# Down projection in stages of 4 plain tiles and 16 tiles by Strassen pairs, a last stage by token halves, and a final scaling by four tiles at a time

## The chip, the cores and the metric

The kernel runs on one core of one Trainium2 chip. The metric is the device time in microseconds (us) of one execution. A core has five engines that run their own instruction queues: TensorE (PE; its weight loads are listed as PEld), VectorE (DVE), ScalarE (ACT), GpSimd (POOL) and SyncE (SP, which here only issues transfers). All transfers run on 16 shared DMA engines.

## The reference

One layer of an encoder over 512 tokens of width 2048 in float32. The change touches only its last step, the SwiGLU feed-forward part with 5632 hidden features and the normalization behind it:

```python
u = rms_norm(h, ffn_pre_g[l])
gate, up = jnp.split(u @ w_gate_up[l], 2, axis=-1)
f = (jax.nn.silu(gate) * up) @ w_down[l]
h = h + rms_norm(f, ffn_post_g[l])
```

`rms_norm` divides each token by the root of its mean square and multiplies by a gain per feature. The output is float32, (1, 512, 2048).

## The kernel before

Activations are held transposed: a tile has 128 features on the partitions and 512 tokens along it. So the hidden activations are 44 tiles (`FT`), the output is 16 tiles (`KT`). `A` and `B` are the first and the last 256 tokens.

**Products of three terms.** Each float32 operand is split into a rounded part `hi` (a ScalarE cast) and the rest `lo` (a VectorE subtraction). A product of one weight tile and one activation tile is three matmuls: hi by lo, hi by hi, lo by hi (`gemm`, lines 179, 182 and 183, whose weights come through `wchunk`, lines 131 to 133). Activations are split by `split` (line 142).

**Pairs.** `strassen` makes two output tiles over 16 contraction tiles at once, by seven products of half size in place of eight (Strassen's scheme in Winograd's form). The operands on the activation side, `op`, are 56 tiles that `prepare` makes: `merged` puts the hi and lo parts of a half side by side (lines 155 and 156), so that the hi weights take one matmul of 512 columns (line 262) and the lo weights one of 256 (line 264). The weights come as four quarters on SP's queue, and one sum of quarters is built by an accumulating DMA on GpSimd's queue (`sums`, line 227). `behind_last` is a function that is called behind the last of the seven products, and the copy of the second result (`done`) then comes behind it.

**Storage.** Tiles named `slot` come from a pool of 66 buffers, weights from three small pools (`raw` 5 buffers, `whi` and `wlo` 3 each), and PSUM has 8 banks (`bank` and `abank`, 4 each). The program is written in order, and a planner orders each engine's instructions from that order and its own estimates; `tc.keep_in_program_order` holds an instruction to the written order on its engine. Waits are made by the framework.

**The work around the change.**
1. Lines 826 to 846 make the hidden tiles 5 to 43 by pairs of gate and up. `activated` stores each tile to `a_d`; for tiles 4 to 19 it also sums their squares (line 796, on GpSimd). At tile 21 the reciprocal root per token is made (`rstd`, then `by_column`, which spreads it over the partitions) as `arow`, its inverse as `irow`. `scaled` loads one of the tiles 4 to 19, multiplies it by `arow` on GpSimd and stores it to `as_d`, so that the pairs' differences work on numbers of one size; one call per tile, from 22 to 37.
2. Plain tiles 0 to 3, for all 16 outputs (`pd0`): a copy of each result (`yf`, line 877, three buffers) is stored to `y_d` from ScalarE's queue. `prepare` runs beside it and loads the scaled tiles (`load_rows`, line 856).
3. Eight pairs over tiles 4 to 19; `added` multiplies each result by `irow` on GpSimd (line 887) and adds it to `y_d` with an accumulating DMA (line 888).
4. Plain tiles 20 to 43, 14 outputs, two at a time (`pd1`): the sum so far is loaded from `y_d` and added on VectorE (line 934), and the squares of the result are summed.
5. The last two outputs in two token halves (`products`, tile names `pl` and `wl`). While the second half's products run, the first half is normalized and stored: `r4` is the reciprocal root, `normalized` (line 956) multiplies by it and by the gain, then h (`ha`, loaded in four-tile and two-tile pieces) is added on GpSimd or VectorE (line 985).
6. The second half: for each two outputs, two multiplications on VectorE from PSUM (line 956), one addition of `hb` (line 997) and one store on SP's queue (line 998).

Of the kernel before, what the change touches and what calls it, by code (L numbers as in the profile page):

```python
# [50 lines left out]
DN_F = 4  # L51
DN_S = DN_F + KT
DN_R = FT - DN_S
# [7 lines left out]
EARLY, EARLY_AT, MORE = 3, 2, 5  # L61
# [6 lines left out]
def hybrid_block(ctx: ExitStack, tc, xT, vecs, rpb, mask, w_c0, w_qk, w_v, w_gg, w_cg, w_ao, w_co, w_out, w_g0, w_gu, w_dn, outT):  # L68
# [717 lines left out]
    asum = const.tile([P, NT], F32, name="asum")  # L786
# [28 lines left out]
    as_d = dr.tile([KT, P, NT], F32, name="as_d")  # L815
    y_d = dr.tile([KT, P, NT], F32, name="y_d")
    arow, irow = asum, const.tile([P, NT], F32, name="irow")

    def scaled(k):

        t = slot(f"an{k}")
        nc.gpsimd.dma_start(t, a_d[DN_F + k])
        nc.gpsimd.tensor_tensor(out=t, in0=t, in1=arow, op=ALU.mult)  # L823
        nc.gpsimd.dma_start(as_d[k], t)

    for j in range(5, FT):
        if j == FT - EARLY_AT:
            acts = [load(k) for k in range(EARLY)]
        c11, c12, c21, c22 = strassen(w_gu[j], w_gu[FT + j], op, f"f{j}", j)
# [16 lines left out]
        activated(j, t)  # L846


    b11, b2, b_t12, b_t34 = [], [], [], []

    rows = []

    def load_rows(c):
        rows.append([slot(f"da{c}_{n}") for n in range(2)])
        for n, t in enumerate(rows[c]):
            nc.gpsimd.dma_start(t, as_d[c + n * HT])

    def prepare(c):

        if c + 2 < HT:  # L860
            load_rows(c + 2)
        u1, u2 = rows[c]
        b11.append(merged(u1[:, A], f"d11_{c}"))
        b2.append([merged(u2[:, cols], f"d2{c}_{n}") for n, cols in enumerate((A, B))])
        tt = stp.tile([P, 2, NT], F32, tag="S", name=f"dt{c}")
        winograd_t(u1, u2, tt[:, 0], tt[:, 1])
        b_t12.append([merged(tt[:, 0, cols], f"d12{c}_{n}") for n, cols in enumerate((A, B))])
        b_t34.append([merged(tt[:, 1, cols], f"d34{c}_{n}") for n, cols in enumerate((A, B))])

    acts += [load(k) for k in range(EARLY, DN_F)]  # L870
    for c in range(2):
        load_rows(c)
    for o in range(KT):
        ps = (bank, abank)[o % 2](f"pd0_{o}")
        gemm([(ps, w_dn[o])], acts, f"wd0_{o}", n=DN_F, pin=o < 2)
        t = stp.tile([P, NT], F32, tag="quad", name=f"yf{o}", bufs=3)
        nc.scalar.copy(t, ps)
        nc.scalar.dma_start(y_d[o], t)
        if o % 2 == 0:
            prepare(o // 2)  # L880


    op = operands(b11, b2, b_t12, b_t34)

    def added(ys):
        for o, t in ys:
# [3 lines left out]
    def split_first():  # L890
        acts.extend(split(t, f"fa{DN_S + k}", pin=True) for k, t in enumerate(first))

    acts = []
    for o in range(0, KT, 2):
# [11 lines left out]
        if o < KT - 2:  # L906
            added(ys)
# [176 lines left out]
```

## Time and profile before

| | |
|---|---|
| three runs, median (lowest to highest) | 2552.57 us (2551.17 to 2553.13) |
| the profiled execution | 2550.88 us |
| its span, first to last instruction | 2549.1 us |
| granted TensorE clock, mean | 0.994 of full |
| moved by DMA | 430.32 MB, 169 GB/s over the span |

The span is one execution as the hardware profiler recorded it. Busy times count instructions, so a busy TensorE can still be one whose matmuls run at a lower clock or wait inside. In the timeline a row is the start, the duration, the engine, the line, the operation with its output and inputs, and the count when several were merged; in brackets stand the idle time before it and what ended it. A matmul's duration is longer than the distance to the next matmul's start, because matmuls overlap; the distance is what one costs in a row of many.

### The profile page before, as it was taken

How to read it: one execution, taken by the hardware profiler on the slowest of the kernel's cores; microseconds unless marked ns; L12 is line 12 of the kernel's file. 1: busy time of each engine (PE TensorE's matmuls, PEld its weight loads, DVE VectorE, ACT ScalarE, POOL GpSimd, SP SyncE). 2: the span in 40 equal slices, each digit the busy share in tenths (PEclk: the TensorE clock that was granted, in tenths of full speed). 3: DMA queues.
4: the chain of work that ended last, by engine and by line, in shares of the span. 5: the costliest groups of instructions: out<-in, count | busy, mean ns of one | idle time of the engine just before them, and what ended most of it. 6: DMA issues, size and time to landing. Idle time of an engine off the chain costs nothing.

```text
span 2549.1 us, 34640 instructions
## 1 busy us (share of the span) xinstructions
PE 2513.1 (99%) x13207; PEld 2158.5 (85%) x13207; DVE 1867.8 (73%) x2412; ACT 1123.1 (44%) x1652; POOL 341.5 (13%) x383
## 2 busy tenths in 40 slices
PE   9999999999999999999999999999999999999997
PEld 7888888878888888889988888888888878878887
DVE  5999896577776655338798888788888888873326
ACT  5223333455554422225455555555555575452222
POOL 0110222220000011001101111112110012330002
PEclk9999999999999999999999999999999999999998
DMA  6246333476667445227356656676666577773335
GB/s 210 91 147 200 107 96 101 157 242 191 189 182 250 153 134 190 97 94 223 103 150 178 184 168 171 180 212 206 199 193 191 175 241 198 185 261 109 115 116 165
DMA packets 143910, 430.32 MB, mean 169 GB/s; under 512 B 16896, under 2 KB 24192, under 8 KB 143744
## 3 DMA queue, kind: packets, MB, share of 16 engines
q1 hardware_dynamic: 102144, 324.32, 38.5%
q0 software_dynamic: 22016, 69.22, 12.7%
q10 hardware_dynamic: 19584, 34.58, 3.7%
q8 instruction: 103, 1.69, 0.3%
q14 instruction: 63, 0.52, 0.1%
HBM read 371.95 MB, written 49.28 MB: 165 GB/s over the span
## 4 chain that ended last, share of the span: by engine, by line
PE 85%; DVE 8%; issue 3%; DMA 2%; ACT 1%; POOL 1%; ACTq 0%; SPq 0%; DVEq 0%; POOLq 0%
PE f L262 19%; PE f L264 10%; PE g L262 7%; PE d L262 4%; PE g L264 4%; PE pd L183 3%; PE pd L179 3%; PE pd L182 3%; PE qk L183 2%; PE qk L182 2%; PE qk L179 2%; PE po L183 2%; PE po L182 2%; PE po L179 2%; PE py L179 2%
## 5 line engine op out<-in xcount | busy, mean ns | idle before, releaser
L408 DVE SCALAR_TENSOR_TENSOR cv<-z,vec,cv 128x497 f32<-128x497 f32 (+14 forms) x240 | 190.7, 796 | 4.8
L133 DVE TENSOR_TENSOR wlo_wd<-raw_wd,whi_wd 128x1024 fp32r<-128x1024 f32 (+1 forms) x58 | 64.2, 1110 | 110.8 <-ACT whi_wd L132 109.4
L132 ACT CAST whi_wd<-raw_wd 128x1024 fp32r<-128x1024 f32 (+1 forms) x58 | 54.0, 934 | 166.5 <-PE pd L182 121.3
L133 DVE TENSOR_TENSOR wlo_wo<-raw_wo,whi_wo 128x1024 fp32r<-128x1024 f32 x36 | 47.4, 1318 | 106.6 <-ACT whi_wo L132 106.5
L132 ACT CAST whi_wo<-raw_wo 128x1024 fp32r<-128x1024 f32 x36 | 37.9, 1054 | 130.0 <-PE po L182 122.7
L320 POOL TENSOR_TENSOR r_r<-r_v,mhalf 128x2 f32<-128x2 f32 (+1 forms) x6 | 7.0, 1174 | 488.7 <-DVE r_v L318 438.2
L132 ACT CAST whi_y<-raw_y 128x1024 fp32r<-128x1024 f32 x32 | 33.5, 1051 | 79.4 <-PE py L182 76.2
L132 ACT CAST whi_qk<-raw_qk 128x1024 fp32r<-128x1024 f32 x32 | 33.7, 1052 | 77.1 <-PE qk L182 56.5
L133 DVE TENSOR_TENSOR wlo_qk<-raw_qk,whi_qk 128x1024 fp32r<-128x1024 f32 x32 | 40.3, 1260 | 32.3 <-ACT whi_qk L132 32.1
L133 DVE TENSOR_TENSOR wlo_y<-raw_y,whi_y 128x1024 fp32r<-128x1024 f32 x32 | 53.3, 1667 | 10.8 <-ACT whi_y L132 9.9
L665 DVE TENSOR_TENSOR gg<-py,gg 128x512 f32<-128x512 f32 x32 | 21.9, 690 | 52.7 <-PE py L183 52.7
L796 POOL TENSOR_TENSOR asum<-asum,asq 128x512 f32<-128x512 f32 x15 | 19.9, 1328 | 237.9 <-ACT asq L795 237.9
L183 PE MATMUL py<-ych,wlo_y 128*128 128x512 f32 x128 | 49.8, 389 | 0.0
L182 PE MATMUL py<-ych,whi_y 128*128 128x512 f32 x128 | 49.8, 389 | 0.0
L179 PE MATMUL py<-ycl,whi_y 128*128 128x512 f32 x128 | 49.8, 389 | 0.0
L842 ACT ACTIVATE sg<-sg 128x512 f32<-128x512 f32 x39 | 24.7, 634 | 50.9 <-DVE sg L300 50.9
L489 POOL TENSOR_TENSOR bm<-braw,msk 128x128 f32<-128x128 f32 x56 | 41.9, 781 | 15.4 <-DMA braw<-in_rpb 15.3
L934 DVE TENSOR_TENSOR y<-pd,y 128x512 f32<-128x512 f32 x14 | 9.7, 691 | 41.6 <-PE pd L183 38.8
L823 POOL TENSOR_TENSOR an<-an,asum 128x512 f32<-128x512 f32 x16 | 25.5, 1594 | 103.8 <-DMA an<-a_d 101.9
L887 POOL TENSOR_TENSOR ys<-ys,irow 128x512 f32<-128x512 f32 x16 | 27.1, 1692 | 76.6 <-PE d L262 41.6
L161 PE MATMUL f<-b,whi_f 128*128 128x256 f32 x128 | 36.4, 285 | 0.8 <-DVE b L156 0.8
L162 PE MATMUL f<-b,whi_f 128*128 128x256 f32 x128 | 36.2, 283 | 0.0
(3077 smaller groups left out, 8492.6 us busy)
## 6 DMA issues: line engine op xcount, KB each, us to landing
raw_wd<-in_w_dn SPq DMA_DIRECT2D x42, 512.0 KB, 3.7
raw_wo<-in_w_out SPq DMA_DIRECT2D x36, 512.0 KB, 3.9
raw_qk<-in_w_qk SPq DMA_DIRECT2D x32, 512.0 KB, 3.7
a_d<-sg ACTq DMA_DIRECT2D x44, 256.0 KB, 3.8
raw_v<-in_w_v SPq DMA_DIRECT2D x16, 512.0 KB, 4.3
raw_y<-in_w_ao SPq DMA_DIRECT2D x16, 512.0 KB, 3.8
gg<-g_d SPq DMA_DIRECT2D x32, 256.0 KB, 4.2
raw_y<-in_w_co SPq DMA_DIRECT2D x16, 512.0 KB, 3.5
```

The costliest lines, as they stand in the source:

```text
L132: cast(hi[:, s], raw[:, s])
L133: nc.vector.tensor_tensor(out=lo[:, s], in0=raw[:, s], in1=hi[:, s].bitcast(F32), op=ALU.subtract)
L161: nc.tensor.matmul(o, hi, t[:, B], start=first, stop=False, skip_group_check=True)
L162: nc.tensor.matmul(o, hi, t[:, A], start=False, stop=False, skip_group_check=True)
L179: mmul = nc.tensor.matmul(ps, hi[:, s], al, start=first, stop=False)
L182: nc.tensor.matmul(ps, hi[:, s], ah, start=False, stop=False)
L183: nc.tensor.matmul(ps, lo[:, s], ah, start=False, stop=last)
L262: nc.tensor.matmul(ps, hi[:, ws[k]], t, start=first and k == 0, stop=False, skip_group_check=True)
L264: nc.tensor.matmul(ps[:, A], lo[:, ws[k]], t[:, A], start=False, stop=last and k == HT - 1, skip_group_check=True)
L408: nc.vector.scalar_tensor_tensor(out=a[:, to], in0=z[:, fr], scalar=col(C_WDW, i * CW + w), in1=a[:, to], op0=ALU.mult, op1=ALU.add)
L489: nc.gpsimd.tensor_tensor(out=bm[:, o + i - i0], in0=raw[:, :, i * BC : (i + 1) * BC], in1=msk[:, o + i - i0, None, :].broadcast_to([P, RO ...
L887: tc.keep_in_program_order(nc.gpsimd.tensor_tensor(out=t, in0=t, in1=irow, op=ALU.mult))
```

## The change

- The hidden tiles go through the down projection in five stages: 0 to 3 plainly, 4 to 19 by pairs, 20 to 23 plainly, 24 to 39 by pairs, 40 to 43 by token halves for all 16 outputs.
- Both groups of 16 are scaled, each by its own rows: two sums of squares (`row[0]`, `row[1]`), two reciprocal roots, two inverses. Of the 32 `scaled` calls 22 stand beside the hidden tiles, 10 in the first pairs, two per pair.
- The plain stage and the making of the pairs' operands are one function, `products_and_operands`, called twice. In the second call a result is added to `y_d` by an accumulating DMA on GpSimd's queue; in the first it is stored as before.
- `added` runs at the head of the next pair or stage, and the first three activation tiles of each plain stage are loaded two pairs ahead and split behind the last product of the pair before.
- The last stage: for each two outputs the weights of tiles 40 to 43 are one DMA, split once into slots and used for both halves. Both outputs of a half share one PSUM bank. The squares of the sums are added up over the outputs in halves. In the second half ScalarE also multiplies each result by its gain (`yg`).
- The final scaling multiplies four tiles at a time by the row in PSUM, adds `hb` for two tiles at a time and stores on two queues.

```diff
+DN_P = 4
+DN_A = (DN_P, DN_P + KT)
+DN_2 = DN_P + 2 * KT
+DN_3 = DN_2 + DN_P
...
     def activated(j, t):
         nc.scalar.dma_start(a_d[j], t)
-        if j == DN_F:
-            nc.scalar.activation(asum, t, AF.Square)
-        elif DN_F < j < DN_S:
-            sq = slot(f"asq{j}")
-            nc.scalar.activation(sq, t, AF.Square)
-            nc.gpsimd.tensor_tensor(out=asum, in0=asum, in1=sq, op=ALU.add)
+        for n, k0 in enumerate(DN_A):
+            if j == k0:
+                nc.scalar.activation(row[n], t, AF.Square)
+            elif k0 < j < k0 + KT:
+                sq = slot(f"asq{j}")
+                nc.scalar.activation(sq, t, AF.Square)
+                nc.gpsimd.tensor_tensor(out=row[n], in0=row[n], in1=sq, op=ALU.add)
...
+    def early(k0):
+        raw = [load_raw(k0 + k) for k in range(EARLY)]
+        return lambda: acts.extend(split(t, f"fa{k0 + k}", pin=True) for k, t in enumerate(raw))
...
-        if j == DN_S + 1:
-            ra, va = rstd([asum], KT * P, "ra", eps=TINY)
-            nc.scalar.copy(arow, by_column(ra, "ra"))
-            ia = const.tile([P, NB], F32, name="ia")
-            nc.vector.tensor_tensor(out=ia, in0=va, in1=ra, op=ALU.mult)
-            nc.scalar.copy(irow, by_column(ia, "ia"))
-        if DN_S + 2 <= j < DN_S + 2 + KT:
-            scaled(j - DN_S - 2)
+        for n, k0 in enumerate(DN_A):
+            if j == k0 + KT + 1:
+                ra, va = rstd([row[n]], KT * P, f"ra{n}", eps=TINY)
+                ia = const.tile([P, NB], F32, name=f"ia{n}")
+                nc.vector.tensor_tensor(out=ia, in0=va, in1=ra, op=ALU.mult)
+                inverse.append(ia)
+            elif j == k0 + KT + 2:
+                nc.scalar.copy(row[n], by_column(ra, f"ra{n}"))
+        if DN_A[0] + KT + 2 <= j < DN_A[1] + KT + 2:
+            scaled(j - DN_A[0] - KT - 2)
+        elif j >= DN_A[1] + KT + 2:
+            if j == DN_A[1] + KT + 3:
+                nc.scalar.copy(row[0], by_column(inverse[0], "ia0"))
+            scaled(j - DN_A[0] - KT - 2)
...
+    def products_and_operands(n, k0, add):
...
+        acts.extend([load(k0 + k) for k in range(EARLY, DN_P)])
+        for c in range(2):
+            load_rows(c)
+        added()
+        for o in range(KT):
+            ps = (bank, abank)[o % 2](f"pd{n}_{o}")
+            gemm([(ps, w_dn[o, :, k0 * P : (k0 + DN_P) * P])], acts, f"wd{n}_{o}", n=DN_P, pin=o < 2)
+            t = stp.tile([P, NT], F32, tag="quad", name=f"yf{o}", bufs=3)
+            nc.scalar.copy(t, ps)
+            if add:
+                nc.gpsimd.dma_start(y_d[o], t, accum_op=ALU.add)
+            else:
+                nc.scalar.dma_start(y_d[o], t)
+            if o % 2 == 0:
+                prepare(o // 2)
...
+    def pairs(n, op, k0):
+        for o in range(0, KT, 2):
+            added()
+            if o == KT - 4:
+                behind = early(k0)
+            w0, w1 = (w_dn[o + i, :, DN_A[n] * P : (DN_A[n] + KT) * P] for i in range(2))
+            c11, c12, c21, c22 = strassen(w0, w1, op, f"d{n}_{o}", o // 2, behind_last=behind if o == KT - 2 else None)
+            for _ in range(2 if left else 0):
+                scaled(left.pop(0))
...
+    pairs(0, products_and_operands(0, 0, False), DN_2)
+    nc.scalar.copy(row[1], by_column(inverse[1], "ia1"))
+    pairs(1, products_and_operands(1, DN_2, True), DN_3)
...
+    def weights(o):
+        raw = wraw(f"wl{o}").rearrange("p (n k) -> p n k", n=2)
+        nc.sync.dma_start(raw, w_dn[o : o + 2, :, DN_3 * P :].rearrange("n p k -> p n k"))
+        for i in range(2):
+            w.append(split(raw[:, i], f"wl{o + i}"))
+            y.append(slot(f"y{o + i}"))
+            load_in_order(y[o + i], y_d[o + i])
+
+    def half(n, between={}):
+        cols, other = ((A, B), (B, A))[n]
+        acc = None
+        for o in range(0, KT, 2):
+            if n == 0:
+                weights(o)
+            ps = (bank, abank)[o // 2 % 2](f"pl{n}_{o}")
+            sq = slot(f"ysq{n}_{o}")
+            for i, part in enumerate((other, cols)):
+                hi, lo = w[o + i]
+                for k in range(DN_P):
+                    s = slice(k * P, (k + 1) * P)
+                    ah, al = (t[:, cols] for t in acts[k])
+                    for wt, t in ((hi, al), (hi, ah), (lo, ah)):
+                        nc.tensor.matmul(
+                            ps[:, part], wt[:, s], t, start=k == 0 and t is al, stop=k == DN_P - 1 and wt is lo,
+                            skip_group_check=True,
+                        )
+            between.get(o, lambda: None)()
+            for i, part in enumerate((other, cols)):
+                t = y[o + i][:, cols]
+                nc.vector.tensor_tensor(out=t, in0=ps[:, part], in1=t, op=ALU.add)
+                nc.scalar.activation(sq[:, part], t, AF.Square)
+                if n:
...
+                    nc.scalar.activation(yg[-1][:, (o + i) % 4], t, AF.Copy, scale=col(C_FPOST, o + i))
...
-    for i in range(0, KT, 2):
-        o = wp.tile([P, 2, HN], F32, tag="raw", name=f"o{i}", bufs=5)
-        for m in range(2):
-            normalized(o[:, m], i + m, B)
-        e = nc.gpsimd if i % 8 == 0 else nc.vector
-        e.tensor_tensor(out=o, in0=o, in1=hb[i // 2], op=ALU.add)
-        nc.sync.dma_start(ov[i : i + 2, :, B].rearrange("k p t -> p k t"), o)
+    rb = r4[0][:, None, B].broadcast_to([P, 4, HN])
+    for g in range(KT // 4):
+        t = yg[g]
+        nc.vector.tensor_tensor(out=t, in0=t, in1=rb, op=ALU.mult)
+        for m in range(0, 4, 2):
+            e = nc.gpsimd if g == 0 or g == 2 and m == 0 else nc.vector
+            e.tensor_tensor(out=t[:, m : m + 2], in0=t[:, m : m + 2], in1=hb[g][:, m : m + 2], op=ALU.add)
+            q = nc.scalar if m else nc.sync
+            q.dma_start(ov[4 * g + m : 4 * g + m + 2, :, B].rearrange("k p t -> p k t"), t[:, m : m + 2])
```

More of the change, by code (lines that the diff above doesn't have):

```diff
@@ L60 @@
 SPLIT = 2
[L61 removed]
+EARLY = 3
 UN_EARLY, YA_EARLY = 2, 3
@@ L846, in hybrid_block @@
         activated(j, t)
[L849 to L886, printed above, removed]
-            tc.keep_in_program_order(nc.gpsimd.tensor_tensor(out=t, in0=t, in1=irow, op=ALU.mult))
-            tc.keep_in_program_order(nc.gpsimd.dma_start(y_d[o], t, accum_op=ALU.add))
@@ L921, in hybrid_block @@
-    y = [None] * KT
-    acc, ha = None, []
-    for g in range(KT // 2 - 1):
-        outs = [((bank, abank)[g % 2](f"pd1_{o}"), o) for o in (2 * g, 2 * g + 1)]
-        for _, o in outs:
-            y[o] = slot(f"y{o}")
-            load_in_order(y[o], y_d[o])
-        gemm([(ps, w_dn[o, :, DN_S * P :]) for ps, o in outs], acts, f"wd1_{g}", n=DN_R, more=lambda k: load(DN_S + k), pin=g < 2)
-        if g == 0:
-            added(ys)
-            load_ha()
-        for ps, o in outs:
-            nc.vector.tensor_tensor(out=y[o], in0=ps, in1=y[o], op=ALU.add)
-            acc = sumsq(acc, y[o], f"y{o}")
@@ L936, in hybrid_block @@
-    for o in (KT - 2, KT - 1):
-        y[o] = slot(f"y{o}")
-        load_in_order(y[o], y_d[o])
-    sq = [slot(f"sq{o}") for o in (KT - 2, KT - 1)]
-    r4 = []
-    def products(n, between=()):
-        cols = (A, B)[n]
-        outs = [((bank, abank)[n](f"pl{n}_{o}"), o) for o in (KT - 2, KT - 1)]
-        gemm([(ps[:, A], w_dn[o, :, DN_S * P :]) for ps, o in outs], acts, f"wl{n}", n=DN_R, cols=cols, between=between)
-        for (ps, o), q in zip(outs, sq):
-            nc.vector.tensor_tensor(out=y[o][:, cols], in0=ps[:, A], in1=y[o][:, cols], op=ALU.add)
-            nc.scalar.activation(q[:, cols], y[o][:, cols], AF.Square)
-            if q is sq[0]:
-                folded([acc[0], q], cols)
@@ new lines, in hybrid_block @@
+    pairs(0, products_and_operands(0, 0, False), DN_2)
+    nc.scalar.copy(row[1], by_column(inverse[1], "ia1"))
+    pairs(1, products_and_operands(1, DN_2, True), DN_3)
+    acts.extend([load(DN_3 + k) for k in range(EARLY, DN_P)])
+    added()
+    ha = []
+    for i in range(0, KT - 4, 4):
+        t = stp.tile([P, 4, HN], F32, tag="S" if i else "S1", name=f"ha{i}")
+        tc.keep_in_program_order(nc.gpsimd.dma_start(t, h_d[i : i + 4, :, A].rearrange("k p t -> p k t")))
+        ha.extend(t[:, m] for m in range(4))
@@ new lines, in hybrid_block @@
+    for i in range(KT - 4, KT, 2):
+        t = stp.tile([P, 2, HN], F32, tag="quad", name=f"ha{i}", bufs=3)
+        tc.keep_in_program_order(nc.gpsimd.dma_start(t, h_d[i : i + 2, :, A].rearrange("k p t -> p k t")))
+        ha.extend((t[:, 0], t[:, 1]))
+    w, y, yg, r4 = [], [], [], []
+    def weights(o):
[5 more added lines that the diff above has]
+            load_in_order(y[o + i], y_d[o + i])
@@ L962, in halved @@
+    def halved(n, squares, pin=False):
         r = []
@@ L964, in halved @@
         return (
-            lambda: r.append(rstd(acc + sq[1:], D, f"r4{n}", blocks, pin)),
+            lambda: r.append(rstd(squares, D, f"r4{n}", blocks, pin)),
             lambda: r4.insert(0, by_column(r[0], f"r4{n}", blocks, pin)),
         )
-    products(0)
-    s1, s2 = halved(0, pin=True)
+    s1, s2 = halved(0, half(0), pin=True)
     hb = []
```

105 lines of the change are left out of this document (56 added, 49 removed).

## The prediction

> **What bounds the kernel now.** I read the page first, for the engine that is never free and the chain that ended last.
>
> ```profile
> PE 2513.1 (99%) x13207; PEld 2158.5 (85%) x13207; DVE 1867.8 (73%) x2412; ACT 1123.1 (44%) x1652; POOL 341.5 (13%) x383
> PE 85%; DVE 8%; issue 3%; DMA 2%; ACT 1%; POOL 1%; ACTq 0%; SPq 0%; DVEq 0%; POOLq 0%
> ```
>
> TensorE is busy 99% of the span and is 85% of the chain. So a removed matmul is worth its issue pitch, wherever its operands arrive in time. Next I cut the down projection into its stages with the table of windows (start:end, length, then busy us of PE, PEld, DVE, ACT and POOL, clock, DMA share, GB/s).
>
> ```profile
> 1625.00:1938.00 313.00, 312.46 (x1795) 275.19 (x1796) 260.79 (x287) 163.41 (x223) 57.98 (x64) 1.00 0.67 200
> 1938.00:2040.00 102.00, 102.00 (x586) 89.78 (x585) 84.30 (x99) 54.93 (x77) 6.02 (x8) 1.00 0.59 171
> 2057.15:2104.80 47.65, 45.04 (x195) 35.59 (x194) 45.00 (x109) 35.74 (x88) 0.94 (x2) 1.00 0.70 234
> 2104.80:2261.20 156.40, 156.40 (x898) 137.68 (x897) 131.87 (x134) 80.47 (x109) 52.39 (x54) 1.00 0.75 201
> 2261.20:2272.00 10.80, 10.80 (x50) 8.94 (x49) 8.79 (x11) 4.32 (x8) 7.68 (x11) 1.00 1.03 392
> 2272.00:2284.00 12.00, 9.86 (x37) 7.68 (x36) 6.78 (x10) 6.78 (x11) 2.80 (x4) 0.86 0.99 318
> 2261.20:2495.40 234.20, 230.64 (x1010) 190.19 (x1009) 83.02 (x91) 61.28 (x76) 10.48 (x14) 0.99 0.44 136
> 2495.40:2531.30 35.90, 35.90 (x301) 35.86 (x301) 23.61 (x38) 12.06 (x14) 11.38 (x13) 1.00 0.60 190
> 2531.30:2549.10 17.80, 2.22 (x14) 1.75 (x12) 11.60 (x25) 0.42 (x1) 3.66 (x4) 0.59 0.45 150
> ```
>
> Rows 1 and 2 are the end of the gate/up pairs, with and without scaling beside them. Row 3 is the four plain tiles while the pairs' operands are made: VectorE is busy 45.0 of 47.65 us there, so it, not TensorE, sets that stage's pace. Row 4 is the eight pairs, 19.55 us each, TensorE full. Rows 5 to 7 are the 24 plain tiles for 14 outputs (rows 5 and 6 their start), row 8 the last two outputs by token halves, row 9 the tail.
>
> **Pitches.** A plain tile costs three matmuls per output. From the timeline, the same matmul one chunk of eight tiles later, 24 matmuls on, for 512 and for 256 tokens:
>
> ```profile
> 2300.07 0.39 PE L183 MATMUL pd<-fa20h,wlo_wd 128*128 128x512 f32 x1
> 2305.51 0.39 PE L183 MATMUL pd<-fa20h,wlo_wd 128*128 128x512 f32 x1
> ...
> 2495.45 0.28 PE L179 MATMUL pl<-fa20l,whi_wl 128*128 128x256 f32 x1
> 2498.33 0.28 PE L179 MATMUL pl<-fa20l,whi_wl 128*128 128x256 f32 x1
> ```
>
> 5.44/24 = 0.2267 us at 512 tokens, 2.88/24 = 0.120 us at 256. Sixteen tiles for two outputs are 96 x 0.2267 = 21.76 us plainly and 19.55 us as a pair: 2.2 us saved per pair.
>
> [...]
>
> **The change, stage by stage.** Times run from the first plain product (2057.15) to the last (2531.3).
>
> 1. First plain stage: its matmuls, splits and merges are the same. 47.65 us, as before.
> 2. First pairs: 156.4 us as before. New beside them are ten `scaled` calls, two per pair in the first five: a GpSimd load, multiply and store each. Two per pair is 1 MB in 19.55 us; one per pair raised the DMA share by 0.08 (rows 1 and 2, which also differ by little else), so 0.75 becomes about 0.91, still open. VectorE has 131.87/8 = 16.5 of 19.55 us, so I cost it nothing; the price without that cover is a rival below.
> 3. Second plain stage (new): 16 x 12 x 0.2267 = 43.5 us of matmuls, with the same VectorE work as stage 1, so at least 47.65 us by that row. One thing is worse: the last pair's two GpSimd multiplies fall into it, where VectorE has no slack. What such a multiply does beside VectorE:
>
> ```profile
> 2267.72 3.22 DVE L133 TENSOR_TENSOR wlo_wd<-raw_wd,whi_wd 128x1024 fp32r<-128x1024 f32 x1 [1.24 <-ACT whi_wd L132]
> 2268.22 1.63 POOL L887 TENSOR_TENSOR ys<-ys,irow 128x512 f32<-128x512 f32 x1
> 2273.20 1.23 DVE L133 TENSOR_TENSOR wlo_wd<-raw_wd,whi_wd 128x1024 fp32r<-128x1024 f32 x1 [1.66 <-ACT whi_wd L132]
> 2274.34 0.68 DVE L142 TENSOR_TENSOR fa29l<-ad,fa29h 128x512 fp32r<-128x512 f32 x1
> 2274.95 0.68 DVE L142 TENSOR_TENSOR fa30l<-ad,fa30h 128x512 fp32r<-128x512 f32 x1
> ```
>
>    The split that met the multiply took 3.22 us, 2 us over its usual 1.23. I take about 0.9 for the pair of multiplies, 48.5 us; the bounds are 43.5 (matmuls alone) and 52 (two such delays in full).
>    Its stores become accumulating DMAs on GpSimd's queue, behind row loads, with the copies to `yf` waiting for them; priced under the rivals.
> 4. Second pairs (new): 8 x 19.55 = 156.4 us. Operands and sums arrive as in row 4.
> 5. Halves: 16 outputs x 4 tiles x 3 x 2 = 384 products x 0.120 = 46.1 us. The old halves, 288 x 0.120 = 34.6 us, took 35.9, so about 1.5 us goes to the first half's statistics between them: 47.6. VectorE in the first half does, per two outputs (2.88 us), two splits, two adds, one sum of squares:
>
> ```profile
> 2254.76 0.69 DVE L142 TENSOR_TENSOR fa20l<-ad,fa20h 128x512 fp32r<-128x512 f32 x1
> 2510.05 0.42 DVE L949 TENSOR_TENSOR y<-pl,y 128x256 f32<-128x256 f32 x1 [0.69 <-PE pl L183]
> 2497.69 0.69 DVE L360 TENSOR_TENSOR y_sq<-y_sq 128x512 f32<-128x512 f32 x1
> 2529.22 0.42 ACT L950 ACTIVATE sq<-y 128x256 f32<-128x256 f32 x1 [5.41 <-DVE y L949]
> ```
>
>    2 x 0.69 + 2 x 0.42 + 0.69 = 2.9 us, just the stage's pace; starts overlap by some 0.08 us each, so 2.5 in fact. ScalarE has 2 x 0.62 + 2 x 0.42 = 2.1. The new gain scaling on ScalarE (nearest row: that 0.42 square) adds 2 x 0.42 per two outputs in the second half, where no splits run. Loads in the first half are 8 x 1.05 MB of weights and sums plus 2.1 MB of h, 10.5 MB; 23 us at row 5's 392 GB/s carry 9.0 MB, so 1.5 MB must be ahead. The five weight buffers alone are 2.6 MB, and fewer activation loads than before (1 in place of 21 behind the early three) compete. I take 1.5 us of stall, bounds 0 and 8. Halves: 49.1 us.
>
> Sum: 47.65 + 156.4 + 48.5 + 156.4 + 49.1 = 458.05, against 474.15 now: **-16.1 us**. Checked another way: the removed plain work is 8 x 2.2 = 17.7 us, halving 48 more products (192 in place of 144) costs 48 x 0.0133 = 0.6, and what the stages take over their matmuls goes from 5.7 + 1.3 (rows 7 and 8 over 1008 x 0.2267 and 34.6) to 5.0 + 3.0: -16.1 again.
>
> 6. Statistics beside the gate/up pairs. Before, one sum and two broadcasts, with a wait for GpSimd between:
>
> ```profile
> 1623.22 0.95 PE L310 MATMUL ra_s<-ones,asum 128*128 128x1 f32 x8
> 1624.03 0.71 PE L262 MATMUL f<-b,f22h 128*128 128x512 f32 x2
> 1625.54 1.16 PE L327 MATMUL ra_b<-ident,ra_r 128*128 128x128 f32 x8 [0.80 <-POOL ra_r L320]
> 1626.53 1.06 PE L327 MATMUL ia_b<-ident,ia 128*128 128x128 f32 x8
> 1627.35 1.64 PE L262 MATMUL f<-b,f22h 128*128 128x512 f32 x6
> ```
>
>    0.81 + 0.80 + 0.99 + 0.82 = 3.4 us. After: two sums and four broadcasts, 1.6 + 3.6 = 5.2 us, the waits gone because each broadcast now comes a pair later. **+1.8 us** (bound +3.4 if two waits stay). The 16 further squares and GpSimd sums, and 22 scalings in place of 16 there, lie beside products: row 1 has ScalarE at 163 and VectorE at 261 of 313 us with TensorE full.
>
> 7. Tail. It begins with the last products, then sum, rstd and broadcast as now.
>
> ```profile
> 2534.49 1.09 PE L327 MATMUL r_b<-ident,r_r 128*128 128x128 f32 x4 [1.04 <-POOL r_r L320]
> 2535.61 2.05 DVE L956 SCALAR_TENSOR_TENSOR o<-y,vec,r_b 128x256 f32<-128x256 f32 x5 [1.96 <-PE r_b L327]
> 2536.62 1.27 POOL L997 TENSOR_TENSOR o<-o,hb 128x512 f32<-128x512 f32 x1 [2.18 <-DVE o L956]
> 2545.35 0.69 DVE L997 TENSOR_TENSOR o<-o,hb 128x512 f32<-128x512 f32 x1
> ```
>
>    VectorE works 2535.61 to 2546.04, 10.4 us, and the last store ends 3.1 us later. After: four multiplies of 1024 columns (nearest row: the split at 2273.20, 1.14 from its start to the next) and five adds of 512 (from 2274.34 to 2274.95, 0.61), 4.6 + 3.0 = 7.6 us; three adds on GpSimd (1.27 each) fit beside. That is -2.8. Given back: a third GpSimd add to collide with, +0.4; and at the end of the products both outputs share a bank and a `yg` scaling stands between the two squares on ScalarE, up to +0.8. I take **-1.8 us**, bounds -2.8 and 0.
>
> Net -16.1 + 1.8 - 1.8 = -16.1; I take off 0.5 for a slow clock behind the new stalls (row 6: 0.86 of full over 12 us with a 2.1 us gap), so **-15.6**. The profiled execution took 2550.88 us (span 2549.1 plus 1.8 around it), the median of the runs is 2552.57, 1.7 above it. So 2535.3 for an execution like the profiled one, **2537 us** as a median.
>
> [...]
>
> **Rivals.**
> - *Exclusion beside the pairs* (same side): in the first five pairs four GpSimd operations run in place of two. Were two more to cost VectorE 1.6 us each, 16.5 + 3.2 = 19.7 passes 19.55, 0.2 to 0.5 us lost per pair, with stage 3 at its bound: +2.5 + 3.5. Time 2543. Against: row 4 already holds two per pair with no gap. Chance 0.11.
> - *Nothing late at all* (same side): no stall in the halves, stage 3 at 45 us: 1.5 + 3.5 + the tail's last 1.0 less. Time 2531 or less. 0.10.
> - *The first half starved by its loads*: 10.5 MB at the 354 GB/s that the window from 2261 to 2284 held is 29.7 us against 23; with the weights of the first outputs late too and a slow clock after the gap (row 6: 0.86), +10. Time 2547, at the edge of no change. For it: row 6, where late splits beside full DMA stalled TensorE. 0.13.
> - *Slower, the accumulating stores of the second plain stage*: three `yf` buffers at 47.65/16 = 2.98 us per output allow 8.9 us from copy to landing. Copy, issue and landing:
>
> ```profile
> y_d<-yf ACTq DMA_DIRECT2D x15, 256.0 KB, 3.3
> y_d<-ys POOLq DMA_DIRECT2D x14, 256.0 KB, 4.2
> y_d<-ys POOLq DMA_DIRECT2D x2, 256.0 KB, 7.2
> da<-as_d POOLq DMA_DIRECT2D x2, 256.0 KB, 9.0
> ```
>
>   4.2 (7.2 under full DMA) + 0.6 + 0.9 is 5.7 to 8.7, just inside. If a store waits behind a row load in GpSimd's queue and is held 13 us, the pitch is 4.33 and the stage 21.7 us longer: 2559. It undoes the gain from a hold of 3 x (2.98 + 0.98) = 11.9 us on. 0.07.
>
> The forecast, 2531 to 2543, has the remaining 0.59. The **range** is 2528 to 2548: it leaves out the store rival and the outer parts of the load and no-stall rivals, some 0.17 in all. A measurement of this kernel can tell about 0.2% (5.1 us) from no change: faster (below 2547.5) 0.59 + 0.11 + 0.10 + half of 0.13, 0.87; the other half, 0.06, the same; slower 0.07.
>
> **What would show it.** Pairs still at 19.55 us; a second plain stage near 48.5 us with VectorE over 90% busy; halves near 49 us; last broadcast to end under 12 us in place of 13.5. Wrong, if the second plain stage shows TensorE waiting for ScalarE's copies (stores), or the first half shows waits for `wl` splits behind DMA.

## The result, and the profile after

The changed kernel takes 2569.23 us (median of 4 runs, 2566.05 to 2570.92) against 2551.87 us (4 runs, 2550.68 to 2553.13): a ratio of 1.0066 with a 95% interval of 1.0049 to 1.0084. It is **slower by 17 us**, where 2537 was forecast with 87 in 100 on faster. The profiled execution is the fastest of the four (2566.05 us, span 2564.3), 15.2 us over the span before.

The page's first line, as that of before: TensorE is called busy 98% of the span, with 200 matmul records more.

```profile
PE 2509.8 (98%) x13407; PEld 2165.6 (84%) x13407; DVE 2010.9 (78%) x2602; ACT 1196.8 (47%) x1838; POOL 466.9 (18%) x504
```

That line would not betray a loss. The table of windows does, cut at the first and last matmul of each stage (start:end, length, busy us of PE, PEld, DVE, ACT and POOL, clock, DMA share, GB/s): first plain stage, first pairs, second plain stage, second pairs, halves, tail. Ahead of row 3 stands the broadcast of the second inverse, 0.8 us.

```profile
2056.87:2108.59 51.72, 47.08 (x195) 37.64 (x193) 45.39 (x109) 36.35 (x89) 7.02 (x12) 0.93 0.76 263
2108.59:2265.00 156.41, 156.41 (x897) 137.76 (x896) 139.05 (x137) 79.00 (x108) 73.87 (x73) 1.00 0.82 228
2265.82:2318.28 52.46, 46.98 (x195) 37.42 (x194) 44.73 (x107) 35.31 (x88) 22.33 (x30) 0.93 0.89 227
2318.28:2474.68 156.40, 156.40 (x897) 137.69 (x895) 131.47 (x136) 77.78 (x106) 46.83 (x42) 1.00 0.74 193
2474.68:2545.20 70.52, 56.06 (x398) 53.10 (x396) 39.48 (x80) 25.45 (x62) 15.80 (x19) 0.90 0.47 155
2545.20:2564.30 19.10, 2.43 (x14) 1.90 (x12) 12.62 (x18) 1.78 (x5) 7.10 (x7) 0.61 0.40 137
```

| stage | forecast, us | measured | off by |
|---|---|---|---|
| first plain stage | 47.65 | 51.72 | +4.1 |
| first pairs | 156.4 | 156.41 | 0.0 |
| second plain stage | 48.5 | 52.46 | +4.0 |
| second pairs | 156.4 | 156.40 | 0.0 |
| halves | 49.1 | 70.52 | +21.4 |
| tail | 16.0 | 19.10 | +3.1 |

With the statistics 1.3 us under the forecast and the 0.5 us that it held back for a slow clock (the clock's cost is inside the rows here), these make the 30.8 us between -15.6 and +15.2. The pairs are exactly as forecast. Two thirds of the miss are the halves, in which no engine is busy all the time: TensorE 56.06 of 70.52 us, VectorE 39.48, ScalarE 25.45, the DMA share 0.47.

**The halves.** What TensorE waited for from 2470 us on (line, releaser: us in total, times, longest):

```profile
PE r_s L312 <- DVE ysq L988: 2.9, 1, 2.9
PE pl L974 <- ACT wl4h L144: 2.3, 1, 2.3
PE pl L974 <- ACT wl2h L144: 1.5, 1, 1.5
PE pl L974 <- ACT wl0h L144: 1.5, 1, 1.5
PE pl L974 <- ACT wl8h L144: 1.5, 1, 1.5
PE pl L974 <- ACT wl10h L144: 1.5, 1, 1.5
PE pl L974 <- ACT wl12h L144: 1.5, 1, 1.5
PE pl L974 <- ACT wl6h L144: 1.5, 1, 1.5
PE pl L974 <- DVE wl0l L144: 1.4, 1, 1.4
```

It waited for the cast of the weights in seven of the first half's eight pairs of outputs, and in the last four of those seven (`wl6h` to `wl12h`) by 1.47 us each time. A wait that repeats to a hundredth points to a loop and not to a late transfer. One turn of it in the timeline, ScalarE's rows first, then VectorE's, then TensorE's:

```profile
2503.60 0.42 ACT L982 ACTIVATE ysq<-y 128x256 f32<-128x256 f32 x1 [3.33 <-DVE y L981]
2503.93 0.60 ACT L144 CAST wl8h<-raw_wl 128x512 fp32r<-128x512 f32 x1
2504.43 0.41 ACT L982 ACTIVATE ysq<-y 128x256 f32<-128x256 f32 x1
2504.75 0.60 ACT L144 CAST wl9h<-raw_wl 128x512 fp32r<-128x512 f32 x1
...
2503.14 0.76 DVE L981 TENSOR_TENSOR y<-pl,y 128x256 f32<-128x256 f32 x2 [1.77 <-PE pl L974]
...
2504.58 0.39 PE L974 MATMUL pl<-fa40l,wl8h 128*128 128x256 f32 x1 [1.47 <-ACT wl8h L144]
2509.68 0.39 PE L974 MATMUL pl<-fa40l,wl10h 128*128 128x256 f32 x1 [1.47 <-ACT wl10h L144]
```

The cast of `wl8` needs only a buffer whose load was issued 35 us before (2468.79) and was in by 2477.5 (none of the eight loads of `raw_wl` took over 8.7 us to land), but it stands in ScalarE's queue behind the square of output 6. That square waits for VectorE's add, and the add for the products of outputs 6 and 7. So the products of the next two outputs cannot start before those of the last two are done, added (2503.14), squared (2503.60) and the cast is made (2503.93 to 2504.5). One turn is 5.10 us (2504.58 to 2509.68) for 2.88 us of products. `weights(o + 2)` is written behind the squares of `o`, and the planner kept that order. The first three turns were longer (7.6, 7.3 and 8.2 us), with matmuls at a lower clock on top (0.71 granted over the three). In one place a transfer was late too: the adds of outputs 2 and 3 waited for their sums from `y_d`, to 2489.83 and 2491.88, which made the waits for `wl4` 1.5 us longer (2.27 and 0.96 us in place of 1.47 and 0.22); all of the turn behind them ran at 0.21 us a matmul.

**The plain stages.** Here too it was the order on ScalarE (kernel 7 below). Rows of ScalarE in the first plain stage, and the matmul that waited:

```profile
2066.75 1.02 ACT L157 CAST d<-da 128x256 fp32r<-128x256 f32 x3 [0.40 <-DMA da<-as_d]
2067.67 1.32 ACT L157 CAST d<-dt 128x256 fp32r<-128x256 f32 x4
2069.80 0.58 ACT L897 COPY yf<-pd 128x512 f32<-128x512 f32 x1 [0.81 <-DMA y_d<-yf]
2070.28 0.62 ACT L134 CAST whi_wd<-raw_wd 128x512 fp32r<-128x512 f32 x1
...
2070.96 0.50 PE L181 MATMUL pd<-fa0l,whi_wd 128*128 128x512 f32 x1 [3.02 <-ACT whi_wd L134]
```

The cast of the weights came behind operand casts that had waited for scaled rows, and behind a copy that had waited for its buffer's store. Behind this pause and one of 1.22 us two matmuls later (for `wlo_wd`) the matmuls ran at 0.43 us in place of 0.2267 for some 5 us; the window's clock is 0.93.

### The profile page after: what moved, and what is told of

It is laid out like the page before. It is cut to its first block, busy times and chain, and to the rows that moved or that the text cites. A ratio compares the mean times of both kernels' runs of the same rounds, so it can differ in the third digit from the quotient of the medians.

```text
span 2564.3 us, 35709 instructions
## 1 busy us (share of the span) xinstructions
PE 2509.8 (98%) x13407; PEld 2165.6 (84%) x13407; DVE 2010.9 (78%) x2602; ACT 1196.8 (47%) x1838; POOL 466.9 (18%) x504
## 5 line engine op out<-in xcount | busy, mean ns | idle before, releaser
L800 POOL TENSOR_TENSOR row<-row,asq 128x512 f32<-128x512 f32 x30 | 41.1, 1370 | 414.3 <-ACT asq L799 414.3
L912 POOL TENSOR_TENSOR ys<-ys,row 128x512 f32<-128x512 f32 x32 | 55.6, 1739 | 138.0 <-DVE ys L302 83.8
L827 POOL TENSOR_TENSOR an<-an,row 128x512 f32<-128x512 f32 x32 | 51.2, 1603 | 69.2 <-DMA an<-a_d 45.7
L860 ACT ACTIVATE sg<-sg 128x512 f32<-128x512 f32 x39 | 24.7, 634 | 51.2 <-DVE sg L302 51.2
L677 POOL TENSOR_TENSOR gg<-gg,gg 128x512 f32<-128x512 f32 x16 | 20.6, 1288 | 112.2 <-ACT whi_y L134 70.8
L418 POOL TENSOR_TENSOR csum<-csum,cv 128x512 f32<-128x512 f32 x7 | 12.7, 1820 | 144.4 <-DVE cv L410 144.4
L165 PE MATMUL f<-b,wlo_f 128*128 128x256 f32 x128 | 36.3, 283 | 0.0
```

Source lines behind the costliest of these rows:

```text
L800: nc.gpsimd.tensor_tensor(out=row[n], in0=row[n], in1=sq, op=ALU.add)
L827: nc.gpsimd.tensor_tensor(out=t, in0=t, in1=row[k // KT], op=ALU.mult)
L912: tc.keep_in_program_order(nc.gpsimd.tensor_tensor(out=t, in0=t, in1=row[n], op=ALU.mult))
```

## The experiments

Twelve kernels ran. Each diff is against the changed kernel unless it says otherwise, and shows the lines that matter (`...` where others are left out); medians are set against the kernel before, run on the same chip in the same rounds (2551.31 us for the first four, 2550.62 for the next four, 2551.06 for the two after them, 2550.19 for the last two).

**1. The weights one pair of outputs ahead.**

```diff
+AHEAD = 1
...
-                weights(o)
+                for i in range(o and o + 2 * AHEAD, min(o + 2 * AHEAD, KT - 2) + 1, 2):
+                    weights(i)
```

`weights` loads and splits the weights of two outputs and loads their sums, so the loads move ahead with the split.

> The weights of the last stage are loaded and split one pair of outputs ahead of their products, so that on ScalarE the split of the next weights no longer stands behind the squares of the present outputs; nothing else changes. Split-order theory: in the changed kernel the first half goes round a loop of products 2.9 us, add 0.4, square 0.4, split 0.5 and its rest, 5.1 us for two outputs; with the split a pair ahead only the products remain, so the pairs of outputs come 2.9 to 3.5 us apart, the first half falls from 48 us to 26 to 32, and the kernel is 15 to 22 us faster than the changed one, 2548 to 2554. Load theory (the sums from y_d land late because h and the weights take the DMA engines): the order does not help the loads, the first half stays above 42 us and the kernel within 6 us of the changed one.

2557.21 us (9 runs), ratio 1.0024 [1.0015, 1.0034]: 6 us over the kernel before in place of 17, by moving a line. TensorE's waits in the halves are now:

```profile
PE r_s L313 <- DVE ysq L990: 3.0, 1, 3.0
PE pl L976 <- ACT wl8h L145: 2.6, 1, 2.6
PE pl L976 <- ACT wl0h L145: 1.5, 1, 1.5
PE pl L976 <- DVE wl0l L145: 1.4, 1, 1.4
```

The waits of 1.5 us in every turn are gone. The gain, 12 us, lies between the two theories' numbers, because two waits stayed: the start, and one cast behind a square whose sum came late:

```profile
2492.95 0.42 DVE L983 TENSOR_TENSOR y<-pl,y 128x256 f32<-128x256 f32 x1 [3.53 <-DMA y<-y_d]
```

That it is the place of the split that counts, and not the earlier loads, rests on the rows of the loop, where the cast waited for a square and for no load, and on kernel 2.

**2. Half of the residual loaded later**, as a test of late transfers.

```diff
-            nc.sync.dma_start(hb[-1], h_d[i : i + 4, :, B].rearrange("k p t -> p k t"))
+            load_in_order(hb[-1], h_d[i : i + 4, :, B].rearrange("k p t -> p k t"))
```

> The four loads of the second half of h (2.1 MB) are held behind all loads of the sums from y_d on SP's queue, where the changed kernel issues them just ahead of the first sums; the order of the splits stays. Load theory: the sums of the second and third pair of outputs land several us earlier and the first half gains most of its loss, 12 to 20 us. Split-order theory: only the part of the first three rounds that exceeds 5.1 us can go (they took 7.6, 7.3 and 8.2 us), so 0 to 7 us, and the later rounds stay at 5.1 us.

2572.06 us (4 runs), 1.008 [1.0064, 1.0097]. No gain; the first half (here and below from its first matmul to the sums of its statistics) took 48.2 us against 50.25, and its later turns kept their 1.5 us. The third turn, behind the late sums, did fall from 8.2 to 5.3 us, while the first rose from 7.6 to 8.5. So late transfers were some 2 us of what the half loses, as long as the order is as it is.

**3. The accumulating stores of the second plain stage taken away**, the rival that would have been slower.

```diff
+    y2_d = dr.tile([KT, P, NT], F32, name="y2_d")
...
-                nc.gpsimd.dma_start(y_d[o], t, accum_op=ALU.add)
+                nc.scalar.dma_start(y2_d[o], t)
```

> The second plain stage stores its products plainly from ScalarE's queue into a buffer of its own and they are not added, so tiles 20 to 23 are left out of the output. Store theory: of the 52.5 us of this stage about 4 come from ScalarE waiting for a product buffer that an accumulating transfer still holds (5.9 us of such idle time), so the stage falls to 47 to 49 us, the kernel by 3 to 6 us. Rival (operand making sets the pace, as in the first plain stage, which took 51.7 us with plain stores): the stage stays at 51 to 53 us and the kernel within 2 us.

2574.57 us (4 runs), 1.0096 [1.0079, 1.0113]; the stage took 53.0 us against 52.46. ScalarE idles 5.9 us for those stores in the changed kernel; without them the stage was no shorter, so they did not set it. This rival is out. The total is 5 us over the changed kernel's, more than either theory allowed; 2 us of that are the first half, 52.4 us in this execution.

**4. Four `scaled` calls fewer at the end of the hidden tiles**, so that GpSimd's queue is free for the rows.

```diff
-        elif j >= DN_A[1] + KT + 2:
+        elif DN_A[1] + KT + 2 <= j < FT - 4:
...
-    left = list(range(FT - DN_A[0] - KT - 2, 2 * KT))
+    left = list(range(FT - 4 - DN_A[0] - KT - 2, 2 * KT))
```

> The scaling calls beside the last four hidden tiles (40 to 43) move into the first pairs, which then have 14 calls, two beside each of seven pairs. Theory: the first plain stage lost 4 us (51.7 against 47.65) because the last scaling calls hold GpSimd's queue, so that its loads of the scaled rows come later and share full DMA engines; without them the stage returns to 47 to 49 us and the first pairs stay at 19.55 us each, the kernel 3 to 5 us faster. Rival (the plain stage is slower because the splits of the activations now stand elsewhere, behind the last product): the stage stays above 51 us.

2571.42 us (4 runs), 1.0079 [1.0064, 1.0094]. The first plain stage fell from 51.72 to 49.35 us; it took 51.5 to 52.0 us in the six other kernels that leave its order alone (1, 2, 3, 5, 6 and 9). So late rows were part of its loss. The total shows nothing of it, and could not: in this execution the first half took 55.1 us against 50.25 with the same order of casts (how far it spread with this loop is in the last section). Inconclusive in the total, clear in the stage.

**5. Weights two pairs ahead, and the residual late.** The edits of 1 and 2, with

```diff
-AHEAD = 1
+AHEAD = 2
```

> Edit: the weights of the first half are emitted two pairs of outputs ahead instead of none, and the loads of the residual's second half stay behind the sums' loads. Of the first half's 36.9 us with one pair ahead, 23 are products; what was left were 2.9 us of waits on the first weights with half the clock behind them (about 3 us), and one wait of 2.6 us on the weights of the ninth output, whose split stood behind a square that waited for a late sum, again with slow matmuls behind it (about 2.5 us). If ScalarE's order alone sets the half, two pairs ahead with the sums early takes the second of these away: 2552 to 2554 us. If the sums' loads set it, whatever the order of the splits, it stays at 2557.

2551.1 us (10 runs), 1.0005 [0.9995, 1.0014]: level with the kernel before, where the changed kernel was 17 us over it. The first half went to 33.1 us. That is 6 us less than kernel 1, and the late cast of `wl8` is gone. Which of the two steps did it, the weights one pair further ahead or the residual behind the sums, was not tried apart.

**6. The first weights split ahead of the last pair's last product.** Added to 5:

```diff
-        return lambda: acts.extend(split(t, f"fa{k0 + k}", pin=True) for k, t in enumerate(raw))
+        def cut():
+            acts.extend(split(t, f"fa{k0 + k}", pin=True) for k, t in enumerate(raw))
+            if k0 == DN_3:
+                acts.extend([load(DN_3 + k) for k in range(EARLY, DN_P)])
+                weights(0)
+        return cut
...
```

> Edit: as the run before, and the last activation and the first pair of weights are split ahead of the last pair's last product. The start wait of 1.5 + 1.4 us and the half clock that follows it (12 x 2 matmuls and more at 0.21 instead of 0.12 us) go: 4 to 6 us less than the run before, if the start is what the products wait for; no gain, if the first sums then make the second pair of outputs wait instead.

2556.7 us (7 runs), 1.0023 [1.0012, 1.0034]: 5.6 us slower than 5, a miss. The start wait did go. But two of VectorE's rows show what took its place:

```profile
2492.30 0.42 DVE L989 TENSOR_TENSOR y<-pl,y 128x256 f32<-128x256 f32 x1 [4.77 <-DMA y<-y_d]
2500.35 0.42 DVE L989 TENSOR_TENSOR y<-pl,y 128x256 f32<-128x256 f32 x1 [3.71 <-DMA y<-y_d]
```

The sums' loads are interleaved in SP's queue with weight loads that wait for a raw buffer, and that wait now came earlier in the list. The adds were late, and the remainders of the next weights (`wl7l`, `wl10l`) stood behind them: 2.9 and 2.8 us on TensorE.

**7. The plain stages' weights two outputs ahead**, the order of the queues there.

```diff
+        cut = [wchunk(w_dn[o, :, k0 * P : (k0 + DN_P) * P], f"wd{n}_{o}") for o in range(2)]
         for o in range(KT):
-            gemm([(ps, w_dn[o, :, k0 * P : (k0 + DN_P) * P])], acts, f"wd{n}_{o}", n=DN_P, pin=o < 2)
+            gemm([(ps, None)], acts, f"wd{n}_{o}", n=DN_P, pin=o < 2, cut=cut[o])
+            if o + 2 < KT:
+                cut.append(wchunk(w_dn[o + 2, :, k0 * P : (k0 + DN_P) * P], f"wd{n}_{o + 2}"))
...
```

> Edit to the changed kernel, in the two plain stages alone: the weights of an output are loaded and split two outputs ahead of its products, so that their cast on ScalarE stands ahead of the copies and the operands' casts. If the plain stages lose their 4 us each because that cast stands behind casts that wait for late rows, both stages come to 44 to 46 us in place of 51.7 and 52.5, and the time to 2555 to 2559. If the rows themselves come too late for the operands, PE waits at the start of the pairs instead, and the time stays within 3 us of 2569.

2567.61 us (4 runs), 1.0068 [1.0053, 1.0083], level with the changed kernel. The stages came to 47.8 and 47.0 us, 9.3 less together, and the pairs gave 3.9 back at their starts (158.1 and 158.6 us against 156.4 each). At the first of those starts:

```profile
2106.70 0.57 ACT L900 COPY yf<-pd 128x512 f32<-128x512 f32 x1
2107.17 1.04 ACT L259 CAST d_0h<-d_0q 128x1024 fp32r<-128x1024 f32 x1
...
2108.27 2.90 PE L264 MATMUL d<-d,d_0h 128*128 128x512 f32 x8 [2.03 <-ACT d_0h L259]
```

The first cast for the pairs stands behind the copy of the last output, which waits for the last product. The wait of 2.03 us is still counted in the plain stage's 47.8; what the pairs gave back here is the slower clock behind it (0.93 granted from 2105 to 2110), with the eight matmuls over 2.70 us (2108.27 to the next group at 2110.97) in place of 1.84. Another 4.7 us went in the first half, which took 54.9 us in this execution.

**8. Edits 6 and 7 together, and the tail's four multiplies ahead of its adds.**

```diff
+    for t in yg:
+        tc.keep_in_program_order(nc.vector.tensor_tensor(out=t, in0=t, in1=rb, op=ALU.mult))
     for g in range(KT // 4):
         t = yg[g]
-        nc.vector.tensor_tensor(out=t, in0=t, in1=rb, op=ALU.mult)
```

> Both edits together, and in the tail the four multiplies of VectorE ahead of all its adds (they ran at 1.16 us beside GpSimd's adds, as alone; VectorE's adds took 1.09 beside them in place of 0.65). The sum, if the parts add: the run before the last, less 10 to 14 us for the plain stages and about 1 us for the tail: 2534 to 2540 us, and so below the kernel before by 11 to 17.

2551.95 us (10 runs), 1.0004 [0.9995, 1.0014]. A miss by 12 us and more: "the sum, if the parts add", but parts 6 and 7 had each opened a new wait, and this kernel has both.

**9. The loads in the order of their use**, in the halves alone. Added to 6, with the casts and adds held to the written order and all of the residual (`ha`, then `hb`) on SP's queue behind the rest. These are several edits in one kernel; what each is worth was not tried apart:

```diff
+                if o == 0:
+                    for i in range(2, 10, 2):
+                        load_weights(i)
+                    load_sums(0, 8)
+                elif o < 8:
+                    load_weights(o + 8)
+                    load_sums(2 * o + 4, min(2 * o + 8, KT))
...
+    squares = half(0)
...
+        load_in_order(t, h_d[i : i + 4, :, A].rearrange("k p t -> p k t"))
...
+    s1, s2 = halved(0, squares, pin=True)
```

> Edits to the changed kernel, in the last four tiles alone: weights two pairs ahead, the first pair of them split ahead of the last pair's last product (as in e6_first_early), and now the loads in the order in which they are used: the sums of the first eight outputs ahead of the weights that wait for a buffer, both halves of the residual behind all of them; the casts, their remainders and the first half's adds are kept in that order. Theory: what e6_first_early gave back was sums that came late, because their loads stood behind weight loads that waited for buffers and beside 4 MB of the residual; then the first half has no wait over 1 us and takes 24 to 27 us instead of 38.9, and the time is 2542 to 2547. Rival: 8 MB of weights and sums are still to come at some 375 GB/s from the start of the stage, so the transfers set the half at 30 us or more: 2548 to 2552.

2547.75 us (10 runs), 0.9991 [0.9981, 1.0]; the profiled execution's span is 2544.4. The halves by the table of windows, and the one wait left in them:

```profile
2475.74:2524.40 48.66, 47.83 (x398) 47.42 (x396) 39.63 (x81) 24.14 (x59) 13.17 (x15) 1.00 0.70 225
```

```profile
PE pl L988 <- DVE wl3l L145: 0.8, 1, 0.8
```

48.66 us against 70.52, at full clock, with the same matmuls, VectorE's same 39.5 to 39.6 us and ScalarE's 24 to 25. The transfers of the first half did not set 30 us: its products are done after 24.7 (2475.74 to 2500.46, with a few of the second half's among them). The total came out 0.75 us above the range expected, a quarter of a us short of the rival's; it is the stage that tells the two apart.

**10. The plain stages' order as well.** Added to 9: edit 7, the operands' casts of an output ahead of the copy of its products, the copy of the last output behind the first cast of the pairs, and the tail of 8.

```diff
         product(x, a11, "11", first=True)
+        if behind_first:
+            behind_first()
...
+            if o % 2 == 0:
+                prepare(o // 2)
...
-            if o % 2 == 0:
-                prepare(o // 2)
+            if o < KT - 1:
+                finished()
+            else:
+                late.append(finished)
```

`finished` copies and stores the result of an output; `pairs` passes the late one as `behind_first`.

> The run before, and the plain stages as in e7_plain_order with two more moves: the operands' casts of an output ahead of the copy of its products, and the copy of the last output behind the first cast of the pairs' weights (it stood ahead of it and waited for the last product, so the pairs began 2 us late); and the tail's four multiplies ahead of its adds. Theory (the order of ScalarE's queue is what all three stages lost): the plain stages 46 to 48 us each and no wait over 1 us at the start of the pairs, so 9 to 12 us less than the run before: 2531 to 2537. Rival (VectorE, with 4.5 us per two outputs of 5.4, is full and only moves the wait into the pairs): 4 us less or nothing.

**2532.72 us** (5 runs, 2531.26 to 2535.48), 0.9934 [0.9922, 0.9947]: 18 us under the kernel before and 36 under the changed one. Its six stages, in the same rows as above:

```profile
2060.49:2106.01 45.52, 44.69 (x195) 35.67 (x193) 42.17 (x107) 34.13 (x87) 6.00 (x12) 1.00 0.83 284
2106.01:2262.75 156.74, 156.66 (x897) 137.57 (x896) 140.93 (x139) 80.00 (x109) 76.21 (x74) 1.00 0.83 231
2263.56:2307.84 44.28, 44.13 (x196) 35.97 (x195) 38.58 (x102) 33.57 (x86) 21.28 (x28) 1.00 1.02 262
2307.84:2465.93 158.09, 156.75 (x898) 137.62 (x896) 135.81 (x141) 80.60 (x111) 45.70 (x40) 1.00 0.75 193
2465.93:2514.57 48.64, 47.84 (x398) 47.43 (x396) 39.61 (x81) 24.12 (x59) 13.15 (x15) 1.00 0.70 225
2514.57:2533.30 18.73, 2.27 (x12) 1.89 (x12) 11.52 (x18) 1.74 (x5) 6.61 (x7) 0.61 0.41 140
```

The plain stages are 45.5 and 44.3 us: VectorE, at 42.17 and 38.58 us, did not fill them, and the clock stayed at 1.00. The rival of a full VectorE is out, but for 1.3 us that the second pairs' start waits for their cast.

**11. The same moves in the kernel before**, which has one plain stage. Against the kernel before:

```diff
+    cut, late = [wchunk(w_dn[o, :, : DN_F * P], f"wd0_{o}") for o in range(2)], []
     for o in range(KT):
         ps = (bank, abank)[o % 2](f"pd0_{o}")
-        gemm([(ps, w_dn[o])], acts, f"wd0_{o}", n=DN_F, pin=o < 2)
+        gemm([(ps, None)], acts, f"wd0_{o}", n=DN_F, pin=o < 2, cut=cut[o])
...
+        if o < KT - 1:
+            finished()
+        else:
+            late.append(finished)
...
```

> The same moves in the plain stage (weights two outputs ahead, operands' casts ahead of the copy, last copy behind the pairs' first cast) made to the kernel before, which has one such stage. Theory: its plain stage took 47.65 us against 43.5 of products, and goes to about 45.5 as in e10_all_order: 2 us less than before, 2548 to 2550. So of e10_all_order's 18 us under the kernel before only some 2 are moves that the kernel before could have had too, and some 16 are the change itself with its queues in order. Rival: the moves are worth the same 10 us here as they brought between e9_load_order and e10_all_order; then 2541 to 2544.

2547.42 us (11 runs), 0.9985 [0.9976, 0.9994]: 2.8 us less, the theory's size; the stage went from 47.65 to 43.5 us. So, of the 18.3 us of kernel 10, 2.8 are moves that the kernel before could have had, and some **15.5** (give or take 4, by the two intervals) are the change itself with its queues in order. Only the plain stage's moves were tried in the kernel before; whether its last stage or its tail would gain from such moves is open.

**12. Less in VectorE's queue ahead of the last statistics.** To 10: the multiplies of the first half's last three outputs go behind the second half's last adds.

```diff
-    for step in halved(1, half(1, {2: s1, 4: first_half})):
-        step()
+    last, broadcast = halved(1, half(1, {2: s1, 4: first_half}))
+    last()
+    normalize(range(KT - LATE, KT))
+    broadcast()
...
```

> Edit to e10_all_order: the multiplies of the last three outputs of the first half go behind the second half's last adds and sums on VectorE, into its wait for the column broadcast. Theory: the last statistics come 3.05 us after the last product because 1.8 us of those multiplies stand in VectorE's queue ahead of them (the kernel before waited 1.02); then PE waits 1.0 to 1.6 us there and the time is 1 to 2 us less than e10_all_order's 2532.7. Rival: the moved multiplies only come due behind the broadcast and push the final multiplies: the wait shrinks, the time does not.

2532.89 us (5 runs), 0.993 [0.9916, 0.9944]: no difference to 10 that these runs could tell: the intervals are 3 us wide to each side, the gain expected was 1 to 2. TensorE's wait shrank only from 3.05 us to:

```profile
2515.62 1.05 PE L316 MATMUL r_s<-ones,ysq 128*128 128x1 f32 x8 [2.50 <-DVE ysq L1018]
```

The multiplies held only 0.5 us of it. Ahead of the last adds VectorE still adds up the squares of the outputs before (0.88 and 0.43 us, from 2512.98 on), and then come add, square and add in series. What that chain could be cut to was not tried.

## Why the prediction was wrong, point by point

- **What bounds the kernel** (TensorE, and a removed matmul is worth its pitch "wherever its operands arrive in time"): right, and the condition is what failed.
- **Steps 2 and 4, the pairs**: right to 0.1 us. Neither the ten scalings beside the first pairs nor the GpSimd multiplies slowed them, so the rival of exclusion beside the pairs is out: VectorE's busy time rose from 131.87 to 139.05 us inside an unchanged 156.4. The 1.6 us that it put on VectorE for each operation more is shown by no run: with ten more that rise is 0.7 us each, if all of it is theirs. (The new GpSimd operations took 1.37 to 1.74 us on average by their line.)
- **Step 5, the halves, is the step that failed**: "I take 1.5 us of stall, bounds 0 and 8"; it was 23, of which some 8 us are slower matmuls and not waits (TensorE is busy 56.06 us with them, and 47.83 in kernel 9, with 398 matmuls in both). The step added up each engine's work per two outputs (2.5 us of VectorE, 2.1 of ScalarE, against 2.88 of products) and the bytes, and took what fits to be hidden. The sums were right, as kernel 9 shows with the same busy times in 48.66 us. What they cannot show is the order of each engine's list: it put the next weights' cast behind the square of the present output, and there it ran (2503.93 us behind 2503.60, with its load in by 2477.5). Adds, square and cast then stand in series with the products, 5.10 us a turn. The code that the step priced shows it: `weights(o)` is written at the head of a turn, behind the squares of the one before. Kernel 1 took the loop out by calling it a turn earlier.
- **Its rival of late loads** (2547) came nearest in place, waits for `wl` splits in the first half, and was wrong in cause: holding the residual back alone brought 2 us in the half and nothing in the total (kernel 2). Late sums showed as the next wait once the order was mended (kernels 1 and 6).
- **The slower rival, the accumulating stores** (2559): right in sign, wrong in mechanism (kernel 3).
- **Steps 1 and 3, the plain stages**, mis-sized by 4.1 and 4.0 us, the second just past its bound of 52. Step 1 assumed "as before". But the rows came later, behind `scaled` work in GpSimd's queue (kernel 4: 2.4 us), and the weights' cast stood behind the casts of those rows. Reading the 47.65 us of before as VectorE's limit was wrong as well: the same work fits in 43.5 us (kernel 11) and 44.3 (kernel 10). 45.0 us busy of 47.65 did not show a full queue.
- **Step 6, the statistics**: +1.8 forecast, +0.5 measured (a start 0.28 us earlier, and 0.81 for the broadcast). The first plain product started between 2056.2 (kernel 1) and 2060.8 us (kernel 6) in seven executions whose code ahead of it is the same, so one execution settles nothing here.
- **Step 7, the tail**: -1.8 forecast, +1.3 measured (19.10 against 17.80). From the last product to the statistics 3.1 us passed in place of 1.5, a loss that the step had put at 0.8 at most; and three of VectorE's adds took 1.09 us each beside GpSimd's. With the multiplies first (kernel 10) the tail took 18.73.
- **The sum**: the saving that the stages were said to hold, 16.1 us, is there once the queues are in order: 15.5 by kernels 10 and 11, give or take 4.

## What to carry to other kernels

Work per engine that fits a stage does not bound it (here 2.5 us of VectorE and 2.1 of ScalarE beside 2.88 of products, and 5.10 us a turn): for every wait inside a loop, write down what stands ahead of the awaited instruction on its own queue, and follow that back; if it comes round to the waiting engine, the turn costs the sum and not the maximum. Written order is due order: put casts one or two turns ahead of their use, and loads that wait for nothing ahead of loads that wait for a buffer (kernel 9, with both: halves of 48.66 us in place of 70.52). Mend one queue and the next shows itself, so measure the stage and not only the total: parts that each open a new wait do not add (kernel 8: 2551.95 us, where the sum gave 2534 to 2540).

## What the runs showed of the hardware

**Behind short waits the clock fell to half, and not always.** The prediction held back 0.5 us for a slow clock; the halves alone lost some 8. Two windows in the first half, nearly two of the loop's steady turns in the changed kernel and one in kernel 7, with the same waits of 1.47 and 0.2 us in each turn:

```profile
2500.00:2510.00 10.00, 6.61 (x48) 5.98 (x48) 5.12 (x11) 3.31 (x9) 0.00 (x0) 1.00 0.45 171
```

```profile
2504.50:2511.00 6.50, 4.80 (x25) 4.39 (x25) 2.56 (x6) 1.66 (x5) 0.00 (x0) 0.74 0.00 0
```

At the clock of 1.00 a turn takes 5.10 us, at 0.74 it takes 6.59, with most of its matmuls 0.21 us apart in place of 0.12. The instructions and the order are the same, and what makes one execution slow and another not is not shown; the first half as a whole took between 48.2 and 55.1 us in five executions with this loop. That is the spread in which kernels 2 to 4 could not show 2 us.

At the start of the changed kernel's halves stand two waits of 1.50 and 1.43 us with two matmuls between them, and behind them the matmuls are 0.21 us apart (granted clock 0.50 from 2478.30 to 2480.90). In kernel 7 one wait of 2.03 us stands ahead of the eight matmuls that took 2.70 us in place of 1.84 (the first pairs, above). With 1.47 us of wait in every turn the clock was 0.74 in each of kernel 7's three steady turns from 2498.0 to 2517.5; in the changed kernel's steady turns, with the same wait, it was 1.00. How long a wait must be to lower the clock is not shown.

**The queues.** In the changed kernel's loop no cast whose inputs were ready ran ahead of a square that waited. The weights of `wl6`, `wl8` and `wl10` were in by 2471.6, 2477.5 and 2487.6 us (the loads' issue and 8.7 us) and were cast at 2498.84, 2503.93 and 2509.03, each time 0.3 us behind the start of a square for which ScalarE had stood idle 5.25, 3.33 and 3.35 us.
